# Two squared-ReLU MLPs in seven-product form: which ScalarE copy goes first, P1's collection by ScalarE and an accumulating transfer, and a norm product two chunks later

## The chip, the core and the metric

One core of a Trainium2 chip runs the whole kernel. The metric is the device time of one execution in microseconds (us). The names used here: PE is TensorE, DVE is VectorE, ACT is ScalarE, POOL is GpSimd, SP is SyncE, which here only issues transfers. PSUM is the memory that PE writes its products to, in banks of 128 partitions by 512 fp32 numbers; SBUF is the memory that all engines work in.

## What is computed

An encoder of two layers over 512 tokens of width 1024: a mixer, then an MLP with a squared ReLU, each behind an RMS norm and added to the residual. The first mixer is a stick-breaking attention, the second a gated linear recurrence.

```python
def squared_relu_mlp(h, w1, w2):          # w1: 1024 x 4096, w2: 4096 x 1024
    u = jax.nn.relu(h @ w1)
    return (u * u) @ w2

for layer in range(2):
    h = rms_norm(x, norm_mix[layer])
    x = x + (stick_breaking_attention(h, ...) if layer == 0 else rglru_block(h, ...))
    h = rms_norm(x, norm_mlp[layer])
    x = x + squared_relu_mlp(h, mlp_w1[layer], mlp_w2[layer])
return rms_norm(x, norm_final)
```

All of it is wanted at fp32 accuracy. The kernel gets that from matmuls of a shorter format: each operand is split into a high part `h` (a rounding, made by a CAST on ACT) and a low part `l` (operand minus high part, made by a TENSOR_TENSOR on DVE), and a product is three matmuls, high by high, high by low and low by high.

## The kernel before, in words

**Stages.** In time: attention with its output product (to about 240 us), layer 0's MLP (to about 570), the recurrence with its input and output products (to about 710), layer 1's MLP and the final norm (to the end).

**Quarters of an MLP.** `Mlp` works through the 4096 hidden columns in four quarters (`q4`). A quarter has an "up" part (1024 columns of `w1`, in two halves `p` = 0 and 1) and a "down" part (1024 rows of `w2`, in two groups `g` = 0 and 1). Each is a product of two-by-two blocks in the form that needs seven block products instead of eight, `P1` to `P7` (`PRODUCTS`). A step is one of the seven for one `p` or `g`: 28 steps to a quarter, 14 up and 14 down, except in the first quarter, where the up part is done wholly or half in the plain way. A step is 24 matmuls of 128x256 (in layer 1's down part 12 of 128x512). In the trace the up steps' matmuls have line L1055, the down steps' L1150 (layer 0) and L1223 (layer 1).

**Banks.** Products add up in PSUM over several steps: `P1`, `P6`, `P7` and `P4` in the bank called X, `P5` and `P3` in V, `P2` in W. Between two of them the running sum has to be read, since each partial sum belongs to another block of the result. So a product that adds to a bank must wait until the sum in it has been read. In the up part, ACT reads X and V with a COPY into a tile `u` (`keep` in `leave`). In the down part, `collect` adds the sum to one of four accumulators `c[0]` to `c[3]` in SBUF (`P1` goes to `c[0]`): two TENSOR_TENSORs of 128x512 on DVE in layer 0, and two SCALAR_TENSOR_TENSORs in layer 1, where each token row has a factor `rr`. The down order is

```python
"mid":  "P1 0 P5 0 P1 1 P2 0 P5 1 P6 0 P6 1 P3 0 P3 1 P7 0 P7 1 P2 1 P4 0 P4 1",
"last": "P1 0 P5 0 P1 1 P2 0 P5 1 P2 1 P6 0 P6 1 P3 0 P3 1 P7 0 P7 1 P4 0 P4 1",
```

and `last` is used for layer 1's last quarter alone. The up order is P1 P5 P6 P3 P7 P2 P4, for `p` = 0 and then for `p` = 1.

**Work around a step.** When step i is written, `leave(i - 1)` writes what ACT and DVE do with the sum of the step before, and then `prepare(i + 3)` makes operands ahead: a weight block `b` (or `raw`) is split into `wh` (CAST on ACT) and `wl` (TENSOR_TENSOR on DVE). Some blocks are sums of two: `added` makes these on DVE (`b<-b,b`), or by a transfer from POOL's queue that adds weights from HBM to a block in SBUF (line L1131). In the up part's second half, `split` and `split_slot` also cut the hidden values into halves `bh`/`bl` and `sh`/`sl` for the down part. After `P4` of `p` = 0, `leave` takes ReLU and square of the bank and starts the sums over `u`.

**What sets the order.** PE's order is that of the code. In the MLPs the orders of DVE and ACT are that of the code too: `self.V` and `self.A` are `Ordered`, which chains each instruction behind the one before; nearly all of their work there has the line L793, so it is told apart by its tiles. The orders of SP's and POOL's queues come from a scheduler. [...]

**Buffers named raw.** Three buffers of 512 KB go round (`tag="raw"`): loads of the block `b21` for `P2` (twice in an up part, twice in a down part), in layer 0 the residual's parts `xr` and the norm factors `ms`, and the weight slabs of the recurrence.

**The norm product.** Where layer 0's MLP ends, DVE sums the squares of x in `ssq`, and PE multiplies that by ones (line L1797) to get the mean over the width. This product is put into the recurrence's third input product, `c2`, by `beside(..., {4: norm})`: ahead of the fifth of its eight chunks of three matmuls. `rms`, `inverse` and `scaled` follow on ACT and DVE.

Of the kernel before, what the change touches and what calls it, by code (L numbers as in the profile page):

```python
# [11 lines left out]
F32 = mybir.dt.float32  # L12
# [3 lines left out]
ALU = mybir.AluOpType  # L16
# [48 lines left out]
def hybrid_encoder(  # L65
# [737 lines left out]
    class Mlp:  # L803
# [353 lines left out]
        def times(self, name, g, i, w, ps, new, cols=slice(0, S)):  # L1157
# [4 lines left out]
            for jj in range(2):  # L1162
                h, l = (t[:, jj, block, ts] for t in self.a[g])
                first, last = new and g == jj == 0, g == jj == 1
                for n, (m, y) in enumerate(((h, wh), (h, wl), (l, wh))):
# [3 lines left out]
                    )  # L1169

        def collect(self, name, i, ps, cols=slice(0, S)):
            out, less = self.PRODUCTS[name][4:]
# [61 lines left out]
        def run(self, first, between, end):  # L1234
# [113 lines left out]
            def leave(i):  # L1348
# [5 lines left out]
                if kind == "down":  # L1354
# [4 lines left out]
                    if p:  # L1359
                        for n in range(2):  # L1360
                            self.collect(name, n, bank[n])
                        if not self.mixed and q4 == NQ - 1:
                            end.done(name)
# [14 lines left out]
                if keep is not None:  # L1378

                    self.A.copy(u[keep], three)  # L1380
                if held:
                    prepare(held.pop())
                    if p:
                        self.sums(0, slice(0, 2), slice(1, 4))
# [8 lines left out]
                if name == "P4":  # L1393
                    self.A.activation(u[3], three, AF.Relu)
                    self.square(u[3])
                    if p:
                        last_sums(u, self.SUMS[:2])
                if later:
                    later.pop()()
# [18 lines left out]
                elif name == "P4" and p:  # L1418
                    last_sums(u, self.SUMS[2:3])
                    self.split_slot(p, u[2], 5)  # L1420
                    last_sums(u, self.SUMS[3:])
                    waiting[:] = [(p, u[j], 3 + j) for j in (0, 1, 3)]
                elif name == "P4":
                    self.sums(p, slice(0, 2), slice(1))
                elif name in ("P5", "P6") and p:
                    n = ("P5", "P6").index(name)
                    if i >= opening:
                        self.split(0, n, slice(0, 4), slice(3, 7))
                    elif n:
                        self.sums(0, n)  # L1430
                    else:
                        self.split(0, 1, slice(0, 4), slice(3, 7))

            waiting, later, held = [], [], []

# [280 lines left out]
    with ExitStack() as rctx:  # L1716
# [70 lines left out]
        def product(key):  # L1787
            tag = TURNS[SLABS.index(key)]
            if key == "c2":
                ps[key] = bank(tag)  # L1790
                beside([ws.pop(key)], xgh, xgl, [ps[key]], {4: norm})
            else:
# [363 lines left out]
```

## Time and profile before

| | |
|---|---|
| median of three runs | 1022.13 us (1021.75, 1022.13, 1025.81) |
| the profiled execution | time 1023.06 us, span 1021.0 us, so 2.06 us lie around the span |
| granted TensorE clock | 0.998 over the span |
| PE, weight loads (PEld), DVE, ACT, POOL busy | 99, 90, 86, 69, 17% of the span |
| DMA | 167.39 MB moved, mean 164 GB/s |

The busy time of PE is modelled: a matmul of 128x256 is shown with 0.28 us, while the next starts 0.113 us after it. A wait that is shorter than the difference therefore does not show as idle time, only as a later start. The number to read is the start of each row. A timeline row that merges eight matmuls (x8) lasts seven spacings and one modelled duration.

### The profile page before, as it was taken

Reading aid. Unit: us, or ns where it says so; the run is one execution under the profiler, and the core shown is the slowest. Engines: PE = TensorE matmul, PEld = TensorE weight load, DVE = VectorE, ACT = ScalarE, POOL = GpSimd, SP = SyncE. Lnnn points to the kernel's source line nnn. Section 1 sums busy time; section 2 is a strip of 40 time slices with the busy share of each in tenths; the row PEclk is TensorE's granted clock in tenths of the full one; section 3 lists DMA queues with packets and bytes.
Section 4 is the critical chain, followed back from the end, with each engine's and each line's share of the span. In section 5 each row is a group of like instructions: output and inputs, shape, how many; then the busy total and the mean of one; then the engine's idle time right before and its main releaser. Section 6 shows DMA issues by size and latency. Waiting matters only on the chain.

```text
span 1021.0 us, 17363 instructions
## 1 busy us (share of the span) xinstructions
PE 1011.5 (99%) x6570; PEld 915.6 (90%) x6570; DVE 875.1 (86%) x1183; ACT 701.4 (69%) x1082; POOL 170.5 (17%) x237
## 2 busy tenths in 40 slices
PE   9999999999999999999999999999999999999997
PEld 8888888888899999999999788888988988988986
DVE  7888787847789899799799988999898898898897
ACT  7767676835766774774776799976773763863866
POOL 0454344420000010010110121100010010010012
PEclk9999999999999999999999999999999999999999
DMA  7845454536637767867774676446767667667654
GB/s 229 228 123 146 107 156 102 153 114 252 169 65 195 200 144 203 207 156 205 188 175 86 157 191 172 118 170 201 209 117 204 163 146 199 173 144 203 164 108 114
DMA packets 61460, 167.39 MB, mean 164 GB/s; under 512 B 8000, under 2 KB 15424, under 8 KB 61376
## 3 DMA queue, kind: packets, MB, share of 16 engines
q1 hardware_dynamic: 49856, 125.46, 38.2%
q0 software_dynamic: 11088, 40.38, 24.1%
q8 instruction: 52, 0.85, 0.3%
q10 hardware_dynamic: 432, 0.44, 0.1%
q14 instruction: 32, 0.26, 0.1%
HBM read 141.61 MB, written 6.30 MB: 145 GB/s over the span
## 4 chain that ended last, share of the span: by engine, by line
PE 81%; DVE 7%; ACT 5%; DMA 3%; issue 2%; SPq 0%; POOL 0%; DVEq 0%; ACTq 0%
PE ps_t L1223 8%; PE ps_acc L1055 8%; PE ps_z L1055 7%; PE ps_t L1150 7%; PE ps_acc L1223 4%; PE ps_acc L234 4%; PE ps_acc L236 4%; PE ps_acc L235 4%; PE ps_acc L1150 4%; PE ps_o L1055 4%; PE ps_z L1223 2%; PE ps_t L234 2%; PE ps_t L236 2%; PE ps_t L235 2%; DVE wl L793 2%
## 5 line engine op out<-in xcount | busy, mean ns | idle before, releaser
L793 ACT CAST wh<-b 128x1024 fp32r<-128x1024 f32 x174 | 179.9, 1050 | 121.2 <-DVE b L793 77.2
L793 DVE TENSOR_TENSOR wl<-b,wh 128x1024 fp32r<-128x1024 f32 x174 | 210.5, 1221 | 31.6 <-ACT wh L793 31.3
L1131 POOL DMA_DIRECT2D b<-in_w_dn x40 | 34.9, 873 | 294.6 <-DVE b L793 198.5
L234 PE MATMUL ps_acc<-xgh,wh 128*128 128x512 f32 x192 | 78.3, 408 | 0.0
L793 ACT ACTIVATE u<-u 128x512 f32<-128x512 f32 x103 | 64.9, 632 | 17.0 <-DVE u L793 15.2
L236 PE MATMUL ps_acc<-xgl,wh 128*128 128x512 f32 x192 | 75.2, 392 | 0.0
L235 PE MATMUL ps_acc<-xgh,wl 128*128 128x512 f32 x192 | 75.2, 392 | 0.0
L606 DVE TENSOR_TENSOR_SCAN scan<-keep,later 128x128 f32<-128x128 f32 (+1 forms) x64 | 58.7, 918 | 15.9 <-ACT keep L596 9.9
L1131 POOL DMA_DIRECT2D b<-in_w_up x26 | 22.6, 869 | 294.5 <-DVE b L793 71.6
L793 DVE TENSOR_TENSOR b<-b,b 128x1024 f32<-128x1024 f32 x50 | 61.2, 1224 | 1.3
L610 POOL TENSOR_TENSOR w<-w,scan 128x128 f32<-128x128 f32 (+1 forms) x64 | 53.1, 832 | 53.1 <-DVE scan L606 47.3
L793 ACT CAST wh<-raw 128x1024 fp32r<-128x1024 f32 x52 | 54.3, 1048 | 10.9 <-PE ps_o L236 2.3
L793 DVE TENSOR_TENSOR u<-u 128x512 f32<-128x512 f32 (+1 forms) x89 | 54.9, 617 | 4.1 <-ACT u L793 2.2
L229 DVE TENSOR_TENSOR wl<-raw,wh 128x512 fp32r<-128x512 f32 (+2 forms) x61 | 50.5, 859 | 4.1 <-ACT wh L227 4.0
L793 DVE TENSOR_TENSOR wl<-raw,wh 128x1024 fp32r<-128x1024 f32 x41 | 50.5, 1231 | 2.1 <-ACT wh L793 2.1
L1055 PE MATMUL ps_z<-xgh,wh 128*128 128x256 f32 x216 | 50.9, 279 | 0.3
L227 ACT CAST wh<-raw 128x512 fp32r<-128x512 f32 (+2 forms) x61 | 41.2, 716 | 12.8 <-PE ps_acc L236 7.3
L1055 PE MATMUL ps_acc<-low,wh 128*128 128x256 f32 x192 | 45.0, 277 | 0.0
L793 DVE TENSOR_TENSOR sl<-u,sh 128x512 fp32r<-128x512 f32 (+2 forms) x53 | 38.0, 717 | 7.7 <-ACT sh L793 7.7
L595 ACT ACTIVATE w<-ps_z,rp 128x128 f32<-128x128 f32 (+3 forms) x56 | 29.7, 530 | 21.1 <-PE ps_z L588 18.4
L600 POOL TENSOR_SCALAR_AFFINE_SELECT w<-w 128x128 f32<-128x128 f32 x64 | 32.1, 502 | 71.5 <-ACT w L595 71.3
L236 PEld LDWEIGHTS ps_acc<-xgl,wh 128*128 128x128 f32 x192 | 36.1, 188 | 7.9
(462 smaller groups left out, 3305.9 us busy)
## 6 DMA issues: line engine op xcount, KB each, us to landing
b<-in_w_dn SPq DMA_DIRECT2D x48, 512.0 KB, 4.5
b<-in_w_dn POOLq DMA_DIRECT2D x40, 512.0 KB, 5.7
b<-in_w_up SPq DMA_DIRECT2D x39, 512.0 KB, 4.8
b<-in_w_up POOLq DMA_DIRECT2D x26, 512.0 KB, 5.6
raw<-in_w_dn SPq DMA_DIRECT2D x16, 512.0 KB, 4.7
raw<-in_w_in SPq DMA_DIRECT2D x16, 512.0 KB, 4.3
raw<-in_w_up SPq DMA_DIRECT2D x13, 512.0 KB, 4.5
raw<-in_w_qk SPq DMA_DIRECT2D x12, 512.0 KB, 3.9
```

The lines of the kernel that those rows point to most:

```text
L227: e[0].copy(wh[:, k, :], raw[:, k, :])
L229: e[1].tensor_tensor(wl[:, k, :], raw[:, k, :], f(wh[:, k, :]), ALU.subtract)
L234: PE.matmul(ps, wh, ah, start=start, stop=False)
L235: PE.matmul(ps, wl, ah, start=False, stop=False)
L236: PE.matmul(ps, wh, al, start=False, stop=stop)
L606: V.tensor_tensor_scan(sc[:, S - n : S][:, ::-1], keep[:, :n][:, ::-1], later[:, S - n :][:, ::-1], 1.0, ALU.mult, ALU.max,)
L610: G.tensor_tensor(wt, wt, sc[:, S - n + 1 : S + 1], ALU.mult)
L793: ins = getattr(self.e, name)(*args, **kwargs)
L1055: PE.matmul(ps[:, i * HS : (i + 1) * HS], m, y, start=new and i == k == low == 0 and y is h, stop=(low, i, k) == steps[-1], skip_group_che ...
L1131: G.dma_start(out=unit[b].rearrange("p j n -> p (j n)"), in_=unit["src"](to), accum_op=ALU.add)
L1150: PE.matmul(ps[:, k * HS : (k + 1) * HS], y[:, jj, f0 : f0 + P], a[:, jj, block, :], start=new and n == jj == k == 0 and a is h, stop=ends ...
L1223: PE.matmul(sums[to][i], a[:, j, block, i * P : (i + 1) * P], y[:, j, :], start=new and g == j == n == 0 and a is h, stop=g == j == 1 and ...
```

## The change

**Up part.** The reading of a bank is put ahead of other work of the same engine. After `P4` of `p` = 0, the ReLU, the square and the first sum (`first_sums`) are not written at once, but at the next step's `leave`, behind the COPY of `P1`'s bank. After `P5` of `p` = 1, the cut into halves (`halves`) is written in the next `leave`, behind the COPY of `P6`'s bank. The list `behind_copy` holds them. In layer 1's first, half-plain quarter neither applies.

ACT's order in layer 0's second quarter shows both moves. The tiles: `ps_z` is the bank X of `p` = 1, `ps_acc` that of `p` = 0, `ps_o` the bank V, `wh` and `bh` are high parts.

```order
+L793 COPY u<-ps_z 128x512
 L793 ACTIVATE u<-ps_acc 128x2x256
 L793 ACTIVATE u<-u 128x2x256
-L793 COPY u<-ps_z 128x512
 L793 CAST wh<-b_3963 128x1024
 L793 COPY u<-ps_o 128x512
 L793 CAST wh<-b_3961 128x1024
 L793 CAST wh<-raw 128x1024
-L793 CAST bh<-u 128x1024
-L793 COPY u<-ps_z 128x512
+L793 COPY u<-ps_z 128x512
+L793 CAST bh<-u 128x1024
```

The first COPY (`P1`) goes from behind two ACTIVATEs to ahead of them, the second (`P6`) from behind a CAST to ahead of it. The same stands in the other five quarters that have a whole up part. DVE's order does not change there.

**Down part.** `P1`'s sums, in the six quarters after each layer's first, are no longer added by DVE. `send` has ACT copy the two banks into a tile `sum` (one of the three `raw` buffers), with the row factor in layer 1, and then a transfer of 512 KB on POOL's queue adds `sum` to `c[0]`, within SBUF. In DVE's order of the second quarter of layer 0 two collecting instructions on `c` (the bank is `ps_t`) go:

```order
 L793 TENSOR_TENSOR wl<-b_4197,wh 128x1024
 L793 TENSOR_TENSOR wl<-b_4193,wh 128x1024
-L793 TENSOR_TENSOR c_3170<-c_3170,ps_t 128x512 x2
 L793 TENSOR_TENSOR b_4197<-b_4197,b_4441 128x1024
 L793 TENSOR_TENSOR sl<-u,sh 128x2x256
```

Behind them, the sum of two weight blocks is the next thing that DVE does. In ACT's order at the same place two instructions come in:

```order
 L793 CAST wh<-b_4197 128x1024
 L793 CAST wh<-b_4193 128x1024
+L793 ACTIVATE sum<-ps_t 128x512 x2
 L793 CAST sh<-u 128x2x256
 L793 CAST wh<-b_4197 128x1024
```

They stand ahead of a CAST of hidden values and of the CAST of the weights that DVE sums. On POOL's queue the transfer from `sum` to `c` comes in between two additions of `w_dn` blocks. Since `sum` takes a turn among the `raw` buffers, SP's order changes as well, here in the same quarter (`xr` and `ms` are the residual and the factors, `raw<-in_w_dn` is the block for the last `P2`):

```order
 L1084 DMA b_4195<-in_w_dn 128x1024
-L1123 DMA raw<-in_w_dn 128x1024
 L1084 DMA b_4193<-in_w_dn 128x1024
 L1084 DMA b_4437<-in_w_dn 128x1024
 L1084 DMA b_4439<-in_w_dn 128x1024
-L1589 DMA xr<-away 128x4x256
 L1084 DMA b_4441<-in_w_dn 128x1024
-L1592 DMA ms<-factors 128x512
-L1084 DMA b_4806<-in_w_up 128x1024
+L1123 DMA raw<-in_w_dn 128x1024
+L1623 DMA xr<-away 128x4x256
+L1626 DMA ms<-factors 128x512
```

The `raw` load, `xr` and `ms` each move to a buffer that comes free later, and stand later in the queue.

**Norm product.** `{4: norm}` becomes `{6: norm}`: the product with ones stands six matmuls later in PE's order.

```diff
+        SENT = (0, 1)
+
+        def send(self, name, banks):
+            out, less = self.PRODUCTS[name][4:]
+            t = wpool.tile([P, C, P], F32, tag="raw", name="sum", bufs=3).rearrange("p c f -> p (c f)")
+            for i, ps in enumerate(banks):
+                scale = 1.0 - 2.0 * less
+                if self.mixed:
+                    at = NB * less + out // 2 * 2 + i
+                    scale = self.rr[:, at : at + 1]
+                self.A.activation(t[:, i * S : (i + 1) * S], ps, AF.Identity, scale=scale)
+            self.gained = G.dma_start(
+                out=self.c[out].rearrange("p i n -> p (i n)"), in_=t, accum_op=ALU.add
+            )
...
                     if p:
-                        for n in range(2):
-                            self.collect(name, n, bank[n])
+                        if name == "P1" and q4 and self.layer in self.SENT:
+                            self.send(name, bank)
+                        else:
+                            for n in range(2):
+                                self.collect(name, n, bank[n])
...
                     self.A.copy(u[keep], three)
+                if behind_copy:
+                    behind_copy.pop()()
...
                 if name == "P4":
-                    self.A.activation(u[3], three, AF.Relu)
-                    self.square(u[3])
+                    def fourth(u=u, three=three):
+                        self.A.activation(u[3], three, AF.Relu)
+                        self.square(u[3])
+
                     if p:
+                        fourth()
                         last_sums(u, self.SUMS[:2])
+                    else:
+                        def first_sums():
+                            fourth()
+                            self.sums(0, slice(0, 2), slice(1))
+
+                        behind_copy.append(first_sums)
...
-                elif name == "P4":
-                    self.sums(p, slice(0, 2), slice(1))
                 elif name in ("P5", "P6") and p:
                     n = ("P5", "P6").index(name)
                     if i >= opening:
-                        self.split(0, n, slice(0, 4), slice(3, 7))
+                        def halves(n=n):
+                            self.split(0, n, slice(0, 4), slice(3, 7))
+
+                        if n:
+                            halves()
+                        else:
+                            behind_copy.append(halves)
...
-                beside([ws.pop(key)], xgh, xgl, [ps[key]], {4: norm})
+                beside([ws.pop(key)], xgh, xgl, [ps[key]], {6: norm})
```

More of the change, by code (lines that the diff above doesn't have):

```diff
@@ L1432, in leave @@
                         self.split(0, 1, slice(0, 4), slice(3, 7))
-            waiting, later, held = [], [], []
+            waiting, later, held, behind_copy = [], [], [], []
             def lead():
```

## The prediction

> **What bounds the kernel now.** I read the page first, then the chain of waits, then the timeline around each place that the change touches. The page's parts 1 and 4:
>
> ```profile
> PE 1011.5 (99%) x6570; PEld 915.6 (90%) x6570; DVE 875.1 (86%) x1183; ACT 701.4 (69%) x1082; POOL 170.5 (17%) x237
> PE 81%; DVE 7%; ACT 5%; DMA 3%; issue 2%; SPq 0%; POOL 0%; DVEq 0%; ACTq 0%
> ```
>
> PE is never visibly idle, and the change removes no matmul. So all it can win is the time that PE loses between matmuls, which the modelled busy time hides. The chain shows how much that is. These rows are the first five products of a whole quarter, in layer 0 (second and fourth quarter) and in layer 1 (second, third and fourth); columns: start, duration, what.
>
> ```profile
> 328.44 13.60 PE ps_acc L1055 x120
> ...
> 484.60 13.60 PE ps_acc L1055 x120
> ...
> 783.97 13.75 PE ps_acc L1055 x120
> ...
> 861.54 13.75 PE ps_acc L1055 x120
> ...
> 937.96 13.75 PE ps_acc L1055 x120
> ```
>
> The same matmuls take 937.96 - 861.54 = 76.42 us in layer 1's third quarter, but 861.54 - 783.97 = 77.57 in its second, and (484.60 - 328.44) / 2 = 78.08 in the second and third of layer 0. Against the clean quarter, three quarters lose 1.15 + 2 x 1.66 = 4.47 us. That is nearly all there is to win in the MLPs.
>
> **Where the up part loses.** Timeline of the second quarter of layer 0, `p` = 1, ACT's rows and PE's (start, duration, what):
>
> ```profile
> 351.02 0.59 ACT L793 ACTIVATE u<-ps_acc 128x512 f32<-128x512 f32 x1
> ...
> 352.18 0.57 ACT L793 COPY u<-ps_z 128x512 f32<-128x512 f32 x1
> ...
> 355.02 1.06 ACT L793 CAST wh<-raw 128x1024 fp32r<-128x1024 f32 x1
> 357.04 1.05 ACT L793 CAST bh<-u 128x1024 fp32r<-128x1024 f32 x1 [0.97 <-DVE u L793]
> 358.00 0.57 ACT L793 COPY u<-ps_z 128x512 f32<-128x512 f32 x1
> ```
>
> ```profile
> 351.85 1.07 PE L1055 MATMUL ps_o<-s,wl 128*128 128x256 f32 x8
> 352.80 0.39 PE L1055 MATMUL ps_z<-bh,wh 128*128 128x256 f32 x1
> ...
> 357.46 1.07 PE L1055 MATMUL ps_o<-s,wl 128*128 128x256 f32 x8
> 358.63 0.39 PE L1055 MATMUL ps_z<-xgh,wh 128*128 128x256 f32 x1
> ```
>
> A row of eight lasts seven spacings and one modelled 0.28, so the spacing is (1.07 - 0.28) / 7 = 0.113 us. `P6` could start at 351.85 + 8 x 0.113 = 352.76 and starts at 352.80; `P7` could at 358.37 and starts at 358.63. Both add to `ps_z`, and ACT's COPY of it ends at 352.75 and 358.57. The first matmul behind each wait is also 0.11 us longer (0.39). So a quarter loses 0.04 + 0.11 + 0.26 + 0.11 = 0.52 us here. Both COPYs could have run earlier: the first behind an ACTIVATE of another bank and its square, the second behind a CAST for which ACT first waits 0.97 us.
>
> *New order.* `P1`'s COPY starts where the ACTIVATE now does, at 351.1, and ends at 351.7, 1.0 us before `P6` needs it. `P6`'s COPY runs from 356.1 (the end of the CAST from `raw`) to 356.7, in ACT's wait, 1.7 us before `P7`. What is pushed back are ReLU and square (by one COPY, 0.57 us) and the CAST, which waits for DVE until 357.04 anyway. In a quarter without the stall ACT comes too early for the COPY:
>
> ```profile
> 504.65 1.48 ACT L793 CAST bh<-u 128x1536 fp32r<-128x1536 f32 x1
> ...
> 505.74 0.62 PE L1055 MATMUL ps_z<-xgh,wl 128*128 128x256 f32 x4
> ```
>
> ACT is free at 506.1 and `P1` ends at 506.36, so ACT would wait 0.3 us there with the ReLU, the square and a weight CAST behind it; PE's weights are made some three steps of 2.72 us ahead, so I count that at nothing. Gain of the up part: 0.52 x 3 quarters = 1.6 us.
>
> **Where the down part loses.** The same quarter, DVE, ACT, POOL and PE (a bracket is the idle time before a row and what ended it):
>
> ```profile
> 379.66 1.28 DVE L793 TENSOR_TENSOR c<-c,ps_t 128x512 f32<-128x512 f32 x2
> 380.85 1.22 DVE L793 TENSOR_TENSOR b<-b,b 128x1024 f32<-128x1024 f32 x1
> ...
> 385.52 1.28 DVE L793 TENSOR_TENSOR c<-c,ps_acc 128x512 f32<-128x512 f32 x2
> ```
>
> ```profile
> 376.34 0.61 ACT L793 CAST sh<-u 128x512 fp32r<-128x512 f32 x1
> 382.16 2.00 ACT L793 CAST wh<-b 128x1024 fp32r<-128x1024 f32 x2 [5.21 <-DVE b L793]
> ...
> 386.06 1.99 ACT L793 CAST wh<-b 128x1024 fp32r<-128x1024 f32 x2
> ```
>
> ```profile
> 385.27 1.11 PE L1150 MATMUL ps_t<-sh,wl 128*128 128x256 f32 x8
> 386.35 0.47 PE L1150 MATMUL ps_acc<-bh,wh 128*128 128x256 f32 x2
> ```
>
> DVE runs without a gap. `P3` adds to `ps_acc`, whose first half DVE has collected at 385.52 + 0.64 = 386.16 or just after; PE could start it at 385.27 + 8 x 0.118 = 386.21 and starts at 386.35, with a first pair 0.07 longer. With a like wait at `P6` that is about 0.3 us in each of layer 0's two quarters, and the excess of layer 1's second quarter that the up part leaves, 1.15 - 0.52 = 0.6, is of this kind. Sum: 1.2 us. If `P1`'s collection (the first row, 1.28 us) leaves DVE, all behind it moves 1.2 us ahead, the collection for `P3` too, and the waits are gone.
>
> *What takes its place.* Two ACTIVATEs from PSUM at 0.59 us (the first row quoted for ACT) are 1.2 us; they stand ahead of the CAST of `sh` at 376.34, and ACT idles 5.21 us behind that. So they are covered, and `P6`'s bank is free at 377.6 instead of 380.9. If that cover went, the weight CAST at 382.16 would be late by up to 1.2 us, which is what DVE gives back. The transfer, by the list of DMA issues (its last column: us to landing), the page's DMA queues (packets, MB, share of 16 engines) and POOL's timeline:
>
> ```profile
> wl<-raw POOLq DMA_DIRECT2D x11, 512.0 KB, 5.4
> ...
> q0 software_dynamic: 11088, 40.38, 24.1%
> ...
> 380.15 0.87 POOL L1131 DMA_DIRECT2D b<-in_w_dn  x1 [6.54 <-DVE wl L793]
> ```
>
> `wl<-raw` is the same kind of transfer, SBUF added to SBUF, and lands 5.4 us after its issue. POOL stands idle 6.54 us there, so the issue (0.87) costs nothing, and the sum is in `c[0]` at about 384. The next reader is `P2`'s collection, nine steps of 2.72 us after `P1` (three in `last`, 8 us: just enough). By q0's row 0.52 MB take 0.241 x 1021 x 0.52 / 40.38 = 3.2 us of all DMA engines. [...] The loads moved on SP's queue:
>
> ```profile
> 359.30 0.38 SPq L1589 DMA_DIRECT2D xr<-away  x1
> ...
> 375.70 0.33 SPq L1592 DMA_DIRECT2D ms<-factors  x1
> 385.63 7.33 SPq L1084 DMA_DIRECT2D b<-in_w_up  x4
> ```
>
> With one more tile in the ring, the last `P2`'s block goes out when `xr` does now (about 361, needed for a CAST at 388), `xr` where `ms` is, and `ms` when `sum` has landed, at 384, just ahead of the four `b` loads, which are for the next quarter. I count these at nothing; they lose PE time only from several us of delay on.
>
> **A slow stretch.** The matmul spacing itself was longer for a while (columns: window, its length, then each engine's busy time and count, the clock, the DMA share):
>
> ```profile
> 381.00:431.00 50.00, 50.00 (x425) 49.85 (x424) 43.55 (x46) 27.23 (x33) 4.34 (x6) 1.00 0.77 201
> 484.00:534.00 50.00, 50.00 (x444) 50.00 (x443) 43.63 (x47) 37.45 (x50) 5.21 (x6) 1.00 0.77 189
> ```
>
> 425 matmuls against 444 in 50 us, 118 ns against 113, at the full granted clock (1.00 in both) and the same DMA share: 19 x 0.113 = 2.1 us. It begins where `P6` has just had to wait. It is the rest of layer 0's loss (3.32 - 1.04 - 0.6 = 1.7). No row tells whether it comes in every execution; its ends are 0 and 2.1 us, and since it is one event of unexplained length I take half, 1.0. [...]
>
> **The norm product.**
>
> ```profile
> 574.00 0.39 PE L236 MATMUL ps_t<-xgl,wh 128*128 128x512 f32 x1
> 574.81 1.13 PE L1797 MATMUL ps_z<-ssq,ones 128*128 128x512 f32 x2 [0.42 <-DVE ssq L793]
> ...
> 575.97 0.69 ACT L793 ACTIVATE r<-ps_z,eps_t 128x512 f32<-128x512 f32 x1 [2.44 <-PE ps_z L1797]
> ...
> 586.68 0.69 DVE L793 TENSOR_TENSOR bl<-bt,bh 128x512 fp32r<-128x512 f32 x1
> ...
> 589.41 0.39 PE L1846 MATMUL ps_z<-bh,gh 128*128 128x512 f32 x1
> ```
>
> At 512 columns the spacing is twice 0.113. PE could go on at 574.23 and starts at 574.81: 0.58 us. Six matmuls later is 574.23 + 6 x 0.227 = 575.59, after `ssq` is there. The price is that ACT's `r` and what hangs on it come 0.8 us later. The first that PE needs of that is `bl`, now at 587.37, for the product at 589.41; then 588.15 against 588.83. It holds, by 0.7 us.
>
> **Sum.** 1.6 (up) + 1.2 (down) + 0.6 (norm) + 1.0 (half the stretch) = 4.4 us, on the profiled execution's own 1023.06: 1018.7. That execution stands 0.9 above the median of the runs, 1022.13, which gives 1017.7; I put 1017.9, since each repaired wait may leave a few hundredths.
>
> **Rivals.**
> - *Nothing to see: 1022.* Another wait could come due right behind each one removed. For it: DVE stays the fullest engine beside PE. Against: the clean quarters run the same orders with no wait left, and the margins above are 0.7 to 1.7 us.
> - *More: 1016.6.* All of the stretch goes: 1.6 + 1.2 + 0.6 + 2.1 = 5.5 us, from the median. For it: it starts at a wait that the change removes. Against: it is one event in one execution.
> - *Slower: the added transfer makes `w_dn` blocks late.* The block issued at 380.15 lands some 5.5 us later, at 385.7, and the second CAST of the row at 386.06 reads it; PE wants that product near 395. CAST and `wl` take 1.05 and 1.2, so there are about 6.8 us of room. Behind `sum` on the same queue it loses 3.2 us if the engines share, 5.4 if one waits for the other to land. From 6.8 on each us costs PE one, in six quarters: 8 us late would be 7 us, 1029.
>
> **How the numbers follow.** The forecast, waits gone and part of the stretch, has 0.56; all of the stretch 0.24; nothing to see 0.13; slower 0.07. Half a per cent, 5.1 us, is about what a measurement of this kernel tells from no change. The forecast and "nothing" lie within it, "more" beyond it. So faster 0.24, same 0.69, slower 0.07. The range reaches from the second rival with a little beyond for a second stretch, 1016.0, to no change, 1022.3.
>
> **What would show it.** Right: the three long quarters take 76.2 to 76.6 us; `P6` and `P7` of `p` = 1 start 8 x 0.113 us after the last row of eight of the step before; ACT's idle time ahead of the weight CAST shrinks by the two ACTIVATEs; the ones product has no wait. Wrong: a quarter of layer 1's kind above 77; POOL's or ACT's rows waiting for `c<-sum`; matmuls waiting in the recurrence near 589; or the stretch standing where no wait is near.

## The result, and the profile after

The changed kernel takes 1019.65 us in the median of 20 executions (1017.97 to 1024.81), the kernel before 1023.83 of 20 beside them (1021.67 to 1026.25). The ratio of the two sets is 0.9971, with a 95% interval of 0.9957 to 0.9985: about 3.0 us faster, inside the half per cent. (It lies near the ratio of the means; the medians alone would give 0.9959, for a reason that follows.) The executions of both kernels fall in two groups some 3 to 5 us apart (before, over all comparisons: 51 near 1022.3 and 47 near 1025.4; changed: 18 near 1019.1 and 14 near 1023.8), so a median moves with the share of each group; the section on the two groups comes back to this.

The profiled execution took 1018.96 us, with a span of 1017.3. Of the page, the busy times, the chain's shares, POOL's DMA queue and the new transfer:

```profile
PE 1008.5 (99%) x6570; PEld 914.4 (90%) x6570; DVE 867.6 (85%) x1171; ACT 708.4 (70%) x1094; POOL 176.6 (17%) x243
PE 92%; DVE 3%; ACT 2%; DMA 1%; issue 1%; POOL 0%; ACTq 0%; DVEq 0%
q0 software_dynamic: 11952, 43.52, 25.5%
```

```profile
c<-sum POOLq DMA_DIRECT2D x6, 512.0 KB, 4.8
```

The chain of waits, with the first products of the same quarters as before:

```profile
327.77 13.60 PE ps_acc L1055 x120
...
482.07 13.60 PE ps_acc L1055 x120
...
780.75 13.75 PE ps_acc L1055 x120
...
857.40 13.75 PE ps_acc L1055 x120
...
933.74 13.75 PE ps_acc L1055 x120
```

Layer 1's second quarter is down from 77.57 to 76.65 us, its third from 76.42 to 76.34, and layer 0's second and third together from 156.16 to 154.30. That is 0.92 + 0.08 + 1.86 = 2.86 us in the quarters. 0.67 us more were won ahead of 328 us, where nothing was changed; that is a difference between executions, for e3 below, whose code up to there is that of the kernel before, stands at 327.92.

The up step of layer 0's second quarter, PE's rows:

```profile
351.18 1.07 PE L1055 MATMUL ps_o<-s,wl 128*128 128x256 f32 x8
352.09 0.28 PE L1055 MATMUL ps_z<-bh,wh 128*128 128x256 f32 x1
...
356.62 1.07 PE L1055 MATMUL ps_o<-s,wl 128*128 128x256 f32 x8
357.53 0.28 PE L1055 MATMUL ps_z<-xgh,wh 128*128 128x256 f32 x1
```

`P6` and `P7` now start 8 x 0.113 us behind the row of eight, and no first matmul lasts 0.39. In the down step of the same quarter `P3` starts 8 x 0.113 us behind its row of eight too, where before it came 0.14 us late:

```profile
384.12 1.07 PE L1150 MATMUL ps_t<-sh,wl 128*128 128x256 f32 x8
385.02 0.39 PE L1150 MATMUL ps_acc<-bh,wh 128*128 128x256 f32 x2
```

But 14 us behind `P7`, where the second group of the down step begins, there is a wait that the kernel before did not have. PE's rows, and ACT's:

```profile
370.22 1.07 PE L1150 MATMUL ps_acc<-bh,wl 128*128 128x256 f32 x8
371.31 1.18 PE L1150 MATMUL ps_t<-sh,wh 128*128 128x256 f32 x8
```

```profile
369.31 1.30 ACT L793 ACTIVATE u<-u 128x512 f32<-128x512 f32 x2 [0.41 <-DVE u L793]
370.64 0.62 ACT L793 CAST sh<-u 128x512 fp32r<-128x512 f32 x1
...
380.25 2.00 ACT L793 CAST wh<-b 128x1024 fp32r<-128x1024 f32 x2 [2.99 <-DVE b L793]
```

`P1` of `g` = 1 could start at 370.22 + 8 x 0.113 = 371.13 and starts at 371.31, behind ACT's CAST of `sh`, which ends at 371.26; the row of eight lasts 1.18 instead of 1.07. That is 0.29 us, and the same place costs 0.39 at 449 us and 0.27 at 824. In the kernel before, ACT's CAST and PE's rows there were:

```profile
371.30 0.62 ACT L793 CAST sh<-u 128x512 fp32r<-128x512 f32 x1
...
371.44 1.07 PE L1150 MATMUL ps_acc<-bh,wl 128*128 128x256 f32 x8
372.35 0.84 PE L1150 MATMUL ps_t<-sh,wh 128*128 128x256 f32 x6
```

The quarter's first product starts at 328.27 before and at 327.61 now. Counted from there, `P1` of `g` = 1 started 44.08 us on before and could start 43.52 us on now, while the CAST of `sh` ends 43.65 us on in both. TensorE has come 0.56 us sooner; DVE and ACT, which make `sh` in turn, have not.

### The profile page after: what moved, and what is told of

Read it like the earlier page. It is cut to its first block, busy times and chain, and to the rows that moved or that the text cites. A ratio compares the mean times of both kernels' runs of the same rounds, so it can differ in the third digit from the quotient of the medians.

```text
span 1017.3 us, 17372 instructions
## 1 busy us (share of the span) xinstructions
PE 1008.5 (99%) x6570; PEld 914.4 (90%) x6570; DVE 867.6 (85%) x1171; ACT 708.4 (70%) x1094; POOL 176.6 (17%) x243
## 3 DMA queue, kind: packets, MB, share of 16 engines
q0 software_dynamic: 11952, 43.52, 25.5%
## 4 chain that ended last, share of the span: by engine, by line
PE 92%; DVE 3%; ACT 2%; DMA 1%; issue 1%; POOL 0%; ACTq 0%; DVEq 0%
PE ps_acc L1055 8%; PE ps_t L1239 8%; PE ps_t L1150 8%; PE ps_z L1055 8%; PE ps_acc L234 5%; PE ps_acc L236 5%; PE ps_acc L235 5%; PE ps_o L1055 5%; PE ps_acc L1239 4%; PE ps_acc L1150 4%; PE ps_t L234 2%; PE ps_t L236 2%; PE ps_t L235 2%; PE ps_z L1239 2%; PE ps_z L1150 2%; PE ps_t L628 2%
```

## The experiments

All the quarters in one table, worked out from the starts of the first products in the chain of waits of each profiled execution (us; the two quarters of layer 0 taken together). The last column says whether the spacing of 117.7 ns, of which more below, held in layer 0 until 565 us.

| kernel | layer 0, 2nd + 3rd | layer 1, 2nd | layer 1, 3rd | 117.7 ns to the end |
|---|---|---|---|---|
| before | 156.16 | 77.57 | 76.42 | no |
| e1, up alone | 157.10 | 77.59 | 76.81 | yes |
| e2, sent alone | 157.66 | 77.20 | 76.34 | yes |
| e3, norm alone | 155.80 | 77.58 | 76.45 | no |
| e7, sent + norm | 154.73 | 76.89 | 76.34 | no |
| changed | 154.30 | 76.65 | 76.34 | no |
| changed, again (e10) | 154.16 | 76.63 | 76.34 | no |
| e4, `P7` held back | 153.22 | 76.34 | 76.34 | no |
| e8, residual sooner | 155.14 | 76.62 | 76.34 | yes |
| e5 and e9, both | 153.23 | 76.34 | 76.34 | no |

Layer 0's two quarters are not alike. By the starts of their first products, the second takes 77.94 us before and the third 78.22; in the changed kernel they take 76.45 and 77.85, in e10 76.45 and 77.72.

### The parts alone

*e1, the up step's order alone*: the changed kernel with the other two parts put back.

```diff
-        SENT = (0, 1)
+        SENT = ()
...
-                beside([ws.pop(key)], xgh, xgl, [ps[key]], {6: norm})
+                beside([ws.pop(key)], xgh, xgl, [ps[key]], {4: norm})
```

> Only the up part's order is changed (the bank's COPY ahead of ReLU and of the cut); P1 is collected by DVE, the norm product stands at the fifth chunk. Theory (waits shift to the next late thing): the 0.52 us at P6 and P7 go in the three long quarters, but PE then reaches the down step P1 of g = 1 about 0.5 us earlier while the CAST of sh that it needs comes no earlier, so 0.2 to 0.4 us appear there; the waits at the down step P3 stay or grow. Net 0.3 to 0.9 us faster than before, ratio 0.9992. Rival (the three parts simply add): 1.6 us faster, no wait at P1 of g = 1.

Measured: 1025.92 us, ratio 1.0019 (1.0006 to 1.0032). Slower: the expectation had foreseen new waits, but still a net gain. Nine of the 12 executions lie in the upper group, so part of the ratio is the share of the groups; both groups stand about 1 us above those of the kernel before. Layer 1's second quarter, where no spacing of 117.7 ns disturbs, shows what was lost. `P6` and `P7` of `p` = 1 no longer wait there; PE's rows of its down step:

```profile
837.77 1.07 PE L1239 MATMUL ps_acc<-wl,sh 128*128 128x512 f32 x4
838.97 0.47 PE L1239 MATMUL ps_t<-wh,bh 128*128 128x512 f32 x1
...
843.77 1.08 PE L1239 MATMUL ps_t<-wl,sh 128*128 128x512 f32 x4
844.95 0.47 PE L1239 MATMUL ps_acc<-wh,bh 128*128 128x512 f32 x1
```

Four matmuls at 0.227 us end the step at 837.77 + 0.91 = 838.68; `P6` starts at 838.97 and waits 0.29 us (DVE's adding of that bank, begun at 838.08, is then at work), where the same wait was 0.03 before. `P3` waits 0.26, and a new wait of 0.27 stands at `P1`. The quarter takes 77.59 as before. The third, 76.42 before, takes 76.81, since `P3` waits 0.28 there too, at 921.76. What the up step wins, the down step gives back, and more.

*e2, the sent collection alone*: the changed kernel with the up step's order and `{4: norm}` put back.

```diff
-                if behind_copy:
-                    behind_copy.pop()()
...
-                    def fourth(u=u, three=three):
-                        self.A.activation(u[3], three, AF.Relu)
-                        self.square(u[3])
+                    self.A.activation(u[3], three, AF.Relu)
+                    self.square(u[3])
...
+                elif name == "P4":
+                    self.sums(p, slice(0, 2), slice(1))
...
-                        def halves(n=n):
-                            self.split(0, n, slice(0, 4), slice(3, 7))
...
+                        self.split(0, n, slice(0, 4), slice(3, 7))
...
-                beside([ws.pop(key)], xgh, xgl, [ps[key]], {6: norm})
+                beside([ws.pop(key)], xgh, xgl, [ps[key]], {4: norm})
```

> Only P1's collection is moved to ACT and the accumulating transfer. Theory: DVE is 1.2 us earlier from each P1 on, so the waits at the down steps P6 and P3 (about 1.2 us in three quarters) go and with them the slow stretch behind 380 us (2.1 us) unless another short wait starts one; the up waits of the second quarter of layer 0 (0.52 us) stay, since the first send comes behind them. 1 to 3 us faster, ratio 0.998. Rival (the transfer makes blocks late): ACT or DVE rows waiting for w_dn blocks, no gain or slower.

Measured: 1020.07 us, ratio 0.9977 (0.9959 to 0.9995). The waits at `P6` and `P3` of the down step are gone, those of the up step stand.

*e3, the norm product alone*, in the kernel before:

```diff
-                beside([ws.pop(key)], xgh, xgl, [ps[key]], {4: norm})
+                beside([ws.pop(key)], xgh, xgl, [ps[key]], {6: norm})
```

> Only the norm product moves from the fifth to the seventh chunk. Theory: 0.58 us of wait at the ones product go, the recurrence has no new wait; span 0.6 us less where other differences of the execution are left out, ratio 0.9994. Rival: the later factors give it back at the gates' product or at the next input products, 0.

Measured: 1021.55 us, ratio 0.9990 (0.9974 to 1.0005), 1.0 us with an interval that reaches past zero. Its profiled execution tells more, on another term. The prediction showed 425 matmuls in 50 us, at 118 ns, in layer 0 of the kernel before. The code there is the same in e3; its row for the same window, and PE's wait at the end of it:

```profile
381.00:431.00 50.00, 48.69 (x427) 48.31 (x426) 43.79 (x46) 28.13 (x35) 4.33 (x5) 1.00 0.77 204
```

```profile
430.86 0.39 PE L1055 MATMUL ps_z<-bh,wh 128*128 128x256 f32 x1 [1.23 <-ACT u L793]
```

Here the spacing was 113 ns, and PE got hardly further: 427 matmuls, since `P6` of the third quarter then waited for ACT's COPY, which ended at 430.81. Layer 0's two quarters took 155.80 us against 156.16. The "slow stretch" was not worth 2.1 us but at most 0.36.

What made that COPY late is in ACT's rows of e3, the first from the second quarter, the others from the third:

```profile
334.83 1.05 ACT L793 CAST wh<-raw 128x1024 fp32r<-128x1024 f32 x1
...
414.15 1.05 ACT L793 CAST wh<-raw 128x1024 fp32r<-128x1024 f32 x1 [2.00 <-DMA raw<-in_w_up]
...
430.24 0.57 ACT L793 COPY u<-ps_z 128x512 f32<-128x512 f32 x1
```

In the third quarter ACT stands 2.00 us for the load of a weight block into `raw`; in the second it doesn't wait for that load at all. Each of the eleven profiles of kernels with no work added shows such a wait there, of 1.0 to 2.0 us (1.45 before), and none shows it in the second quarter. So the third quarter's `P6` was 1.39 us late in e3, where the second's was 0.04 late in the kernel before. That the load is the cause is read from the rows; no run here has the block in time.

*e7, everything but the up step's order*: e2 with the norm product where the changed kernel has it.

```diff
-                beside([ws.pop(key)], xgh, xgl, [ps[key]], {4: norm})
+                beside([ws.pop(key)], xgh, xgl, [ps[key]], {6: norm})
```

> The changed kernel with the up step's order put back as before: P1's collection by ScalarE and a transfer, and the later ones product, stay. Theory of the prediction (parts add up): 1.6 us slower than the changed kernel (its waits for the COPY of P6 and P5, 0.52 us in three quarters), so near 1020.6 in the faster executions. Theory from the runs of the parts (they don't add up: the earlier COPY alone was 2.5 us slower in the median than the kernel before, the sent collection alone 3.3 faster): 0.2 to 0.8 us slower than the changed kernel, 1019.2 to 1019.8 in the faster executions, since with the COPY late by 0.52 us the third CAST sh of the down step comes in time, and the 0.27 to 0.39 us that the changed kernel waits for it at 371, 449 and 824 us isn't there. The profile's quarters tell them apart: 76.9 us for the second and third quarter of the second layer if the old waits are all that is there (76.65 and 76.34 in the changed kernel).

Measured: 1021.11 us, ratio 0.9976 (0.9959 to 0.9993); the faster group lies near 1019.8, the changed kernel's near 1019.1. The chain's rows:

```profile
327.99 13.60 PE ps_acc L1055 x120
...
482.72 13.60 PE ps_acc L1055 x120
...
781.41 13.75 PE ps_acc L1055 x120
...
858.30 13.75 PE ps_acc L1055 x120
...
934.64 13.75 PE ps_acc L1055 x120
```

Against e3, the sent collection wins (155.80 - 154.73) + (77.58 - 76.89) + (76.45 - 76.34) = 1.07 + 0.69 + 0.11 = 1.87 us. Up to 0.4 of that is a slow spacing that e3 has in two short stretches, 431 to 437 and 458 to 464 us, and e7 has not. On top of it the up step's order wins (154.73 - 154.16) + (76.89 - 76.63) = 0.83 us against e10, 0.67 against the first profile of the changed kernel. So the parts don't add: the up order is worth about 0.7 to 0.8 us behind the sent collection and less than nothing ahead of it.

### The new wait

*e4*: the changed kernel, with `P7`'s ReLU and square held back by one step, as `P3`'s are, so that ACT and DVE come to the next step's work first.

```diff
-                    if p and name == "P3":
+                    if p and (name == "P3" or name == "P7" and i >= opening):
                         later.append(rest)
```

> The changed kernel, and P7's ReLU, square and cut (p = 1) are written behind P2's sum in the next leave, as P3's are already: DVE adds P2's bank before it waits for P7's sh. Theory (the new wait at the down step P1 of g = 1 is DVE's idle time of 0.62 us ahead of P7's sl, which holds P2's sum and so the next CAST of sh): that CAST comes 0.6 to 1.3 us earlier, the waits of 0.29, 0.39 and 0.27 us go, three quarters at 76.2 to 76.4 us. 0.9 us faster than the changed kernel, ratio to before 0.996. Rival (P1 of g = 1 waits for something else): the wait stays.

Measured: 1018.56 us, ratio 0.9960 (0.9943 to 0.9976). The waits at 371 and 824 us, 0.29 and 0.27 in the changed kernel, are gone, layer 1's second quarter takes 76.34, as long as the clean one, and layer 0's two take 153.22; at 448 us one wait of 0.66 stays.

*e8 and e5/e9*: the residual's second half is added one step sooner, alone (e8) and with e4's edit (e5, and again as e9).

```diff
-            (0, 27): (0, 0), (1, 0): (0, 1), (1, 25): (2, 0), (1, 27): (2, 1),
-            (2, 0): (1, 0), (2, 1): (1, 1), (2, 25): (3, 0), (2, 27): (3, 1),
+            (0, 27): (0, 0), (1, 0): (0, 1), (1, 25): (2, 0), (1, 26): (2, 1),
+            (2, 0): (1, 0), (2, 1): (1, 1), (2, 25): (3, 0), (2, 26): (3, 1),
```

> The changed kernel with the residual's second half added one step sooner alone (P7's relu and square not held back). Theory (holding back P7's relu and square is what takes the new waits at 371, 449 and 824 us away, 0.95 us in all; the buffer freed sooner is worth 0.1 to 0.2 us at 413 us): waits of 0.15 to 0.4 us for the third CAST sh stay at P1 of the down step's second half, the third quarter of the second layer's MLP but one stays near 76.65 us, and the faster executions lie at 1018.6 to 1019.0, with an upper group near 1023. Rival (the sooner addition carries the gain of the combined kernel, 1017.95): no such waits, 1017.9 to 1018.3 and no upper group.

> The changed kernel with P7's relu and square held back by one step as P3's are (the kernel e4, 1018.56 median) and, besides, the residual's second half added one step sooner in the second and third quarter of the first layer, which frees its buffer for the next weight block 2.7 us sooner. In the profile of the changed kernel ScalarE's CAST of that block stood 2.02 us for its transfer at 413 us and made P6's COPY and the next product late by some 20 ns. Theory (that buffer is what is late there): no matmul waits between 404 and 449 us, and the time is 0 to 0.8 us below e4, 1017.8 to 1018.5 in the median, 1017.0 to 1018.0 in the faster executions. Rival (VectorE is full in these quarters, so the addition done sooner makes the next CAST or subtraction late): a wait of 0.1 to 0.7 us appears at the down step's P1 or P5 in the second or third quarter, and the time is that of e4 or up to 0.7 us above.

> The combined kernel once more (P7's relu and square held back and the residual's second half added sooner), since six executions of it, 1017.07 to 1018.45, had none in the upper group that a third to a half of the executions of the other kernels fall in. Theory (without a real wait in the second and third quarter nothing redraws the spacing, so it stays at 113.4 ns): again none above 1020, the median 1017.6 to 1018.3. Rival (six were too few): a quarter to a half of the executions at 1021.5 to 1023.

Measured: e8 1019.97 us, ratio 0.9972 (0.9956 to 0.9989), its three waits in place; e5 1017.95, ratio 0.9931 (0.9914 to 0.9947); e9 1017.87, ratio 0.9957 (0.9942 to 0.9972). The combined kernel has the lowest medians, but its intervals overlap e4's in e9, and its quarters are e4's. ACT stands 1.75 us for the weight block near 413 us in e5 and 1.74 in e4, so the sooner addition did not do what it was meant for. Five of e8's executions lie at 1017.9 to 1018.7, below what was expected of it and below the changed kernel's 1019.1; why is open, since its profile is one of the upper group. Of 13 executions of the combined kernel one was above 1020, of 9 of e4 three. Whether that is more than chance is open, and the reason on record (no wait, so nothing to redraw the spacing) lacks its premise: e9's profile has a wait of 0.65 us at 448.3, and its spacing stayed at 113 ns behind it.

### The two groups

*e10*: the changed kernel once more.

> The changed kernel itself once more, on the chip of the two runs beside it: 1018.0 to 1020 in the faster executions, about a third near 1023.5, ratio to the kernel before 0.996 to 0.998. Theory (the profile's spacing decides the group): if the profiled execution lies near 1019, the spacing of 117.7 ns holds at most between 414 and 449 us; if near 1023.5, it holds from 449 us or sooner to 565 us.

Measured: 1021.20 us, ratio 0.9986 (0.9970 to 1.0003), six of 12 executions at 1019.0 to 1020.0 and six at 1022.4 to 1025.5. The profiled one took 1019.09 and has no slow stretch at all; in the first profile 34 us of the third quarter, 415 to 449, ran at 117.7 ns. Both come to the same place. e10 at that place:

```profile
447.30 1.07 PE L1150 MATMUL ps_acc<-bh,wl 128*128 128x256 f32 x8
449.36 1.18 PE L1150 MATMUL ps_t<-sh,wh 128*128 128x256 f32 x8 [1.00 <-ACT sh L793]
```

The wait for `sh` is 1.16 us here and was 0.28 behind the stretch, with the next matmul 0.11 late in both. Against the 76.16 us that a quarter of layer 0 takes with no wait (the second in e9), the third loses 77.85 - 76.16 = 1.69 us in the first profile, 0.39 of it at that wait and the rest by the spacing, and 1.56 in e10, 1.27 at that wait and 0.28 at `P6` (429 us). Here the slow spacing ahead of the wait was taken out of the wait.

Behind the last wait nothing took it up. A window of the fourth quarter, behind that wait, in e8, whose profiled execution (1022.89) lies in the upper group, and in e10 (columns: window, its length, PE, PEld, DVE, ACT and POOL busy and count, clock, DMA share, GB/s):

```profile
455.00:515.00 60.00, 60.00 (x512) 60.00 (x511) 51.19 (x54) 35.20 (x43) 5.82 (x7) 1.00 0.73 190
```

```profile
455.00:515.00 60.00, 60.00 (x532) 60.00 (x531) 53.14 (x56) 36.46 (x45) 6.11 (x7) 1.00 0.78 199
```

512 matmuls against 532, both at the full granted clock. From the wait at 449 us to the first product of 128x512, e8 needs 113.2 us at 117.7 ns a matmul and e10 108.9 at 113.4: 4.3 us more. The groups of the changed kernel lie 4.7 apart. In the kernel before, the last wait stands at 465 us and the first such product at 561; 95 us x 3.8% = 3.6, and its groups lie 3.1 apart. Of the eleven profiles of kernels with no work added, the three in an upper group (e1, e2, e8) have this spacing up to the products of 128x512, and the eight others do not. What the executions without a profile did can't be seen.

*e6*: waits put where the kernel has none, by copies that repeat what is there.

```diff
                     self.A.copy(u[keep], three)
+                    if self.layer == 0 and q4 == NQ - 1 and name == "P6":
+                        for _ in range(6):
+                            self.A.copy(u[keep], three)
```

> The changed kernel with work added: in the last quarter of the first layer's MLP ScalarE copies the bank of P6 seven times instead of once in each half of the up step (6 x 0.53 = 3.2 us more, twice), so that TensorE has one or two real waits near 493 and 512 us, where it had none between 449 and 565. It costs by itself some 0.5 to 1.5 us of waiting a place. Executions of every kernel so far fall in two groups about 4.4 us apart (changed kernel: near 1019.0 and near 1023.5). Theory (the upper group is the spacing of 117.7 ns, taken up at the last wait, 449 us, and kept to the first product of 128x512 at 565 us: 116 us x 3.8% = 4.4 us; a new wait draws it anew): the two groups break up; the stretches 449 to 493, 493 to 512 and 512 to 565 are drawn apart (1.6, 0.7 and 2.0 us), so that times fill the room between the groups, under one in six lies in the old upper group, and the profile shows the spacing change at the added waits or not at all. Rival (the two groups come from elsewhere: the transfers, the other half of the kernel, the device): both groups move up by the added waits, 1 to 3 us, with 4.4 us between them and nothing in the gap.

Measured: 1025.76 us, 1024.49 to 1028.90 in 12 executions, with no step between neighbours above 1.5 us. The added waits take 4.7 us, so the old groups would lie near 1023.8 and 1028.5; one execution is above 1028. PE's two waits, and windows behind each and further on:

```profile
494.46 0.38 PE L1055 MATMUL ps_acc<-xgh,wh 128*128 128x256 f32 x1 [1.67 <-ACT u L793]
...
516.26 0.38 PE L1055 MATMUL ps_z<-xgh,wh 128*128 128x256 f32 x1 [2.48 <-ACT u L793]
```

```profile
455.00:490.00 35.00, 35.00 (x311) 35.00 (x310) 31.71 (x35) 16.43 (x19) 4.37 (x5) 1.00 0.88 232
497.00:513.00 16.00, 16.00 (x144) 16.00 (x143) 13.15 (x15) 13.54 (x19) 1.73 (x2) 1.00 0.59 117
530.00:565.00 35.00, 35.00 (x295) 34.83 (x294) 34.27 (x49) 23.34 (x31) 3.50 (x4) 1.00 0.64 145
```

The waits were larger than expected (1.9 and 2.8 us). 35 us hold 311 matmuls at first and 295 at the end: the spacing changed not at the added waits but at a third, small one of 0.09 us at 530. Two groups 4.4 us apart no longer show, as the spacing theory expects and the rival (both groups move up together) does not. One reservation: five of the 12 executions had a mean granted clock of 0.996 or 0.997, where those of the kernel before beside them had 0.998 or 0.999, so a part of the spread can be the clock's; the other seven lie at 1024.85 to 1026.38.

*m1 and m2*: the products alone, with waits of chosen length, to see what draws the spacing. The loop of m1 (`block` is 48 products of 128x256, or 24 of 128x512, the first of which reads `y`), and what m2 changes in it:

```python
for r in range(blocks):
    ps = block(y[:, :width], width, first, second)
    y = work.tile([P, S], F32R, tag="y", name="y")
    t = work.tile([P, S], F32, tag="u", name="u")
    A.copy(t[:, :64], ps[:, :64])
    A.mul(idle[:, :1024], idle[:, :1024], 1.0)
    w = LENGTHS[r % len(LENGTHS)]
    A.mul(idle[:, :w], idle[:, :w], 1.0)
    A.copy(y, x[:, r % C, :])
```

```diff
-LENGTHS = [400 + 12 * ((37 * k) % 96) for k in range(96)]
+LENGTHS = [200 + 12 * ((37 * k) % 96) for k in range(96)]
...
-    t = work.tile([P, S], F32, tag="u", name="u")
-    A.copy(t[:, :64], ps[:, :64])
+    A.mul(idle[:, :64], ps[:, :64], 0.01)
...
-    A.copy(y, x[:, r % C, :])
+    A.copy(y, idle[:, :S])
```

> This kernel computes nothing of the reference: TensorE runs 96 blocks of 48 products of 128x256 (own weights each, fp32r) and 24 blocks of 24 products of 128x512, and the first product of each block waits for a ScalarE chain whose last part is made longer or shorter from block to block, so that the waits run from none to about 1 us. It measures by itself what the traces so far show: after a wait TensorE goes on either at 113.4 ns a product or at 117.7, and keeps that spacing until its next wait. Theory (each wait draws the spacing anew, and only products of 128x256 know two): a fifth to a half of the 96 blocks run at 117 to 118.5 ns, the others at 113 to 114, each block the same from its first products to its last, and all blocks of 128x512 at one spacing of 226 to 228 ns. Second theory (the length of the wait decides): the slow blocks are those of one range of waits, below about 0.06 us or some other band, and none lie outside. Rival (the slow spacing comes from other traffic: weight transfers, VectorE, GpSimd): with only ScalarE running beside it no block is slow.

> The kernel of the run before had no wait in it: its chain on ScalarE was not tied to the product by data, so TensorE ran 96 blocks of 48 products of 128x256 without a stop, at 120.0 ns a product for 560 us, and the products of 128x512 at 226.7. Here the chain is tied (each step works on the tile of the step before, and the first product of a block reads the last), so the waits run from none to about 1 us; nothing of the reference is computed. Theory (each wait draws the spacing anew, among 113.4, 117.7 and 120 ns, and products of 128x256 keep it until the next wait): of the blocks behind a wait some run at 113 to 114 ns and a fifth to a half at 117 to 120, each at one spacing from its tenth product on, with no tie to the length of the wait, and blocks of 128x512 all run at 226 to 228. Second theory (the length of the wait decides): the slow blocks lie in one band of waits. Rival (120 ns is simply what this operand layout costs): all blocks run at 120 ns, waits or not.

Both failed to make the waits they were written for. m1 had none: its TensorE ran over 560 us at one spacing, 120.0 ns, with ScalarE alone beside it:

```profile
300.00:400.00 100.00, 100.00 (x836) 100.00 (x835) 0.00 (x0) 28.30 (x49) 0.00 (x0) 1.00 0.00 1
```

So a spacing of 120.0 ns stood here, and was kept, with almost no other traffic: DVE and POOL had no instruction in the window, the DMA share is 0.00, at 1 GB/s. That this is the same thing as the 117.7 ns of the MLP is not shown: m2 gave 120 ns on the mean as well, and the rival on record for it, that 120 ns is what these operands cost, stays open. In m2 the products were put in another order than written, first all that wait for nothing, again at a mean of 120 ns (836 in 100 us at clock 1.00), then with waits between them, 39 us of idle time in a window of 100:

```profile
600.00:700.00 100.00, 60.85 (x302) 57.85 (x301) 0.00 (x0) 35.95 (x52) 0.00 (x0) 0.72 0.00 0
```

There the granted clock was 0.72, and 302 matmuls kept PE busy for 60.85 us, 0.20 us each, so nothing can be read of short waits. What in a wait decides between 113 and 118 ns was not settled: in the kernel before the first matmul of `P6` came 0.156 us behind the one ahead of it, at 352.8, and the spacing was 113 soon after; in e2 the same matmul came 0.157 us behind, and the spacing was 118.

## Why the prediction was right or wrong

- *Up part, 1.6 us: the waits went, the size did not hold.* The waits at `P6` and `P7` are gone but one, and ACT's order is as worked out; the one left is `P6` in layer 0's third quarter, 0.28 us in e10. What failed is the step "0.52 x 3 quarters", in two ways. It priced each wait as if nothing stood behind it in the same quarter. The next thing that PE needs from ACT and DVE, the third `sh`, had less to spare than the time won, and took 0.29 and 0.27 us of it in layer 0's second and layer 1's second quarter. And it took layer 0's third quarter to be like the second, where the load into `raw` made `P6` 1.39 us late in e3; the new order hands nearly all of that on to `sh`, 1.27 us in e10. Measured: 0.7 to 0.8 us behind the sent collection, 0.26 to 0.30 a quarter against e10; alone, a loss. The mechanism is that of the rival "nothing to see", which the prediction put aside with margins of the moved instructions themselves; those margins held but in layer 0's third quarter, and the next product's was not looked at.
- *Down part, 1.2 us: right, and under-sized.* 1.87 by e7 against e3, or some 1.5 if e3's short slow stretches are left out. The waits at `P6` and `P3` are gone; ACT's idle time ahead of the weight CAST went from 5.21 to 2.99 us, by the two ACTIVATEs and because DVE's sum comes sooner, as the prediction said it would.
- *Norm product, 0.6 us: right.* From layer 0's last quarter to layer 1's second, 484.60 to 783.97 in the chain's rows before, 299.37 us went by; in e3 it is 298.64 and in the changed kernel 298.68, 0.7 less. PE's rows show the product without the wait, and the recurrence follows with none:

```profile
572.83 0.39 PE L236 MATMUL ps_t<-xgl,wh 128*128 128x512 f32 x1
573.06 1.02 PE L1831 MATMUL ps_z<-ssq,ones 128*128 128x512 f32 x2
...
585.98 0.39 PE L236 MATMUL ps_o<-xgl,wh 128*128 128x512 f32 x1
586.20 0.39 PE L1880 MATMUL ps_z<-bh,gh 128*128 128x512 f32 x1
```

- *Slow stretch, 1.0 us: wrong.* The step "it is the rest of layer 0's loss" failed. The stretch ended at a wait whose end ACT set, so what it cost was that wait in another form; e3 without the stretch was 0.36 us shorter there. The rest of the loss was the third quarter's late COPY, behind the load into `raw`. The prediction named a stretch with no wait near as a sign against it, and the first profile of the changed kernel has one at 415 to 449, begun at a lateness of some 20 ns. Nor did a wait leave the slower spacing each time: most waits here, among them 1.16 us in e10, were followed by 113 ns. What makes the spacing slower, no run shows.
- *Slower by the transfer: did not come.* `c<-sum` lands in 4.8 us, q0's share went from 24.1 to 25.5%, and the CAST of the weights behind it waits for DVE, not for a transfer. The `w_dn` blocks on the same queue land in 5.7 us in the median on both pages; whether two transfers in flight share the engines, or one waits for the other, no run shows.
- *The sum.* 0.8 + 1.9 + 0.6 and at most 0.4 for the stretch make 3.3 to 3.7 us, against 4.4 predicted; the ratio gives 3.0 (1.5 to 4.4). One term twice too large and one wrong were partly made up by one too small. That the profiled execution came to 1018.96, so near the 1018.7 of the sum, is luck: 0.67 of its 4.1 us were won ahead of 328 us, where nothing was changed. Against the mark of 76.2 to 76.6 us, layer 0's second quarter took 76.45, layer 1's second 76.65, and layer 0's third missed it with 77.85, because of the wait for `sh` and the slow spacing ahead of it.

## What to carry to other kernels

In these quarters, taking a wait away won no more than the slack of the next product that depended on the same engines, so read the whole quarter's next waits before adding terms, and expect parts that unload different engines of one chain to be worth something only together. Don't multiply one quarter's wait by the number of quarters before the same row has been read in each. A stretch in which the matmuls merely run slower cost little here where a wait ended it (1.69 against 1.56 us in one quarter, with and without it); behind the last wait it cost all of it, 4.3 us. Where executions fall in groups, compare profiles of both groups before explaining a median.

## What was unexpected in the hardware

Matmuls of 128x256 in fp32r, with a new weight load each, ran at one of several steady spacings at the full granted clock: 113.4 or 117.7 ns in the MLPs, 120.0 in m1, there for over 560 us without change. Every stretch of 117.7 ns that lasted over 30 us began at a wait or a lateness of tens of ns (some 20 at 415 us in the changed kernel, 90 at 530 us in e6) and ended at a wait or at the first product of 128x512; at that width 31 products in a row took 7.02 us in the changed kernel (584.62 to 591.64), 226.5 ns each. In the eleven profiles this tells the two groups of executions apart, and its 4.3 us make up most of the 4.7 between them. And in m2 a window of 100 us with 39 us of idle time between matmuls had a granted clock of 0.72, where it stood at 1.00 in the windows behind the two waits of 1.9 and 2.8 us that stood alone in e6.
